# The last output projection of a two-layer mixer with tokens as rows: 512 channels per matmul, x turned beforehand, the final norm's weights spread by DMA, and the result sent in two halves of tokens

## The chip, the core and the metric

The kernel runs on one core of one Trainium2 chip. The metric is the device time of one execution in microseconds (us). Three executions of the kernel before took 1207.74, 1208.77 and 1210.25 us; their median, 1208.77 us, is the time before. The profile and the trace come from another execution, which took 1207.9 us.

TensorE (PE) does the matmuls and transposes, VectorE (DVE) and ScalarE (ACT) the element-wise work, GpSimd (POOL) a few powers, and SyncE (SP) issues all DMA transfers. Each engine takes its instructions in the order in which the program wrote them.

## The reference, cut to what matters

```python
def rms_norm(x, w):
    y = x * lax.rsqrt(jnp.mean(x * x, axis=-1, keepdims=True) + NORM_EPS)
    return y * w

def hybrid_layer(x, ...):               # x: 256 tokens x 1024 channels, float32
    h = rms_norm(x, norm_w)
    z = h @ w_in + b_in                 # 20 x 1024 columns: queries, keys, values, gates, convolution
    ...                                 # retention -> y_ret, attention -> y_att, convolution -> y_conv
    merged = gates[0] * y_ret + gates[1] * y_att + gates[2] * y_conv
    return x + merged @ w_out

for l in range(2):
    x = hybrid_layer(x, ...)
return rms_norm(x, final_norm_w)
```

## The kernel before, in words

All products run in a split form: a float32 matrix is taken apart into a high part and a low part, and a product is the sum of three matmuls (high by high, high by low, low by high). The weights arrive in steps of 256 output columns, 96 steps in each layer and 192 in all (`units`, numbered n). A step is named here by its kind and number: the last layer ends with ma2, ma3, then ya0 to ya3 (attention's projection), mc0 to mc3 (a merge gate), cg0 to cg3, yc0 to yc3 (the convolution's projection) and wo0 to wo3 (the output projection `w_out`), steps 164 to 191.

For each step three things are written into the program at different places. `load(n + 3)` stands at the head of step n and lets SP issue the transfer of the weights of step n + 3 into two `raw` tiles (there are five). `split(n + 2)` comes next: ACT casts each raw tile into `whi`, DVE subtracts and writes `wlo` (five of each). Then come the matmuls of step n. So a raw tile is free for a later load when DVE has written the `wlo` of what lay in it. What follows the matmuls is set by tables of due times: `play(inside, n)` in the middle of a step's matmuls, `play(first, n)` and `play(due, n)` behind them. Kinds in `WIDE` are taken two steps at a time (`gemm_wide`): tokens are the rows of the result, 128 at a time, and a matmul yields 512 channels; the first of the two steps covers contraction blocks 0 to 3 and the second 4 to 7, each first for tokens 0 to 127 (t = 0) and then for tokens 128 to 255 (t = 1). 

One dependence crosses these steps. The layer norm of the convolution needs its mean over channels: DVE works out `mean` and two diagonal matrices `dg` during ya3, behind the splits of mc0 and mc1 in DVE's order, and PE multiplies by them in the middle of mc0 (`ln_rows`, the matmul that writes `rb`).

The residual `x` has channels as rows (`xt`, 8 blocks of 128 channels by 256 tokens). The output projection, in both layers, yields channels as rows too (`gemm_two`): 256 columns a matmul. `project_last` adds it to x, multiplies by the final norm's weights (a number for each row here), and `turn_out` transposes the product back to tokens as rows, for the first four blocks in the middle of wo3 and for the others behind it. The sums of squares over channels are matmuls against a column of ones (`token_sums`), one part behind wo3; `rstd` follows on DVE and POOL; ACT and DVE scale the four 128 x 512 pieces of the result, and SP sends each.

Of the kernel before, what the change touches and what calls it, by code (L numbers as in the profile page):

```python
# [10 lines left out]
F32 = mybir.dt.float32  # L11
# [15 lines left out]
W = 256  # L27
# [117 lines left out]
def trunk(ctx: ExitStack, tc, xp, wp, b_in, params, consts, out):  # L145
# [78 lines left out]
    def bank():  # L224
        return ps.tile([128, 2, W], F32, tag="g", name="g", bufs=4)
# [33 lines left out]
    def gemm_wide(n, a, done):  # L259

        hs, ls = hi_t.pop(n), lo_t.pop(n)
        n0, half = couple[n]
        if half == 0:
            st["wide"] = [bank(), bank()]
        for t in range(2):
            p = st["wide"][t]
            if t == 1:
                play(inside, n)
            r = slice(t * 128, t * 128 + 128)
            for c in range(4):  # L270
                k, d = 4 * half + c, slice(2 * (c % 2), 2 * (c % 2) + 2)
                wh, wl = hs[c // 2][:, d, :], ls[c // 2][:, d, :]
                for i, (u, v) in enumerate(((0, wh), (0, wl), (1, wh))):
                    PE.matmul(p, a[:, k, u, r], v, start=(k == 0 and i == 0), stop=(k == NK - 1 and i == 2))  # L274
            if half and t == 0:
                done(0, p)
        return p

    def gemm_two(n, a, done):


        hs, ls = hi_t.pop(n), lo_t.pop(n)
        n0, half = couple[n]
        if half == 0:
            whole = bank(), bank()
            st["two", n0] = [halves(t) for t in whole], whole
            if n0 + 2 == N:
                st["two", n0][0][1][1] = ps.tile([128, W], F32, tag="S", name="g", bufs=4)
        parts, whole = st["two", n0]
        for u in range(2):  # L290
            if u == 1:
                play(inside, n)
            last = n0 + u + 1 == N
            for j, c in ((j, c) for j in range(2) for c in range(4)) if last else ((j, c) for c in range(4) for j in range(2)):
                k, d, t = 4 * half + c, 2 * (c % 2) + u, slice(j * 128, j * 128 + 128)
                for i, (w, v) in enumerate(trio_of(a, k, hs[c // 2][:, d, t], ls[c // 2][:, d, t])):
                    PE.matmul(parts[u][j], w, v, start=(k == 0 and i == 0 and (j == 0 or last)),  # L297
                              stop=(k == NK - 1 and i == 2 and (j == 1 or last)))
            if half and u == 0:
                done(0, whole[0])  # L300
        return parts[1] if last else whole[1]

    def hi_lo(dst, k, v, nk, n=None):

# [13 lines left out]
    def token_sums(tiles, ss=None, more=False):  # L318

        start = ss is None  # L320
        if start:
            ss = ps.tile([128, 2], F32, tag="S", name="ss", bufs=4)
        for q, v in enumerate(tiles):
            for t in range(2):
                PE.matmul(ss[:, t:t + 1], v[:, t * 128:t * 128 + 128], ones[:, 0:1],
                          start=(start and q == 0 and t == 0), stop=(not more and q == len(tiles) - 1 and t == 1))
        return ss
# [381 lines left out]
        later(pos[l + 1, "cs", 0], add_squares, (l + 1, "sq"), xs, i == 0, i == 3, at=first)  # L709


    def turn_out(k):
        if k == 0:
            st["nat"] = [[ps.tile([128, 512], F32, tag="S", name="nat", bufs=4) for _ in range(2)]]
        if k == 4:
            st["nat"].append([bank().rearrange("p a b -> p (a b)") for _ in range(2)])
        for t in range(2):
            PE.transpose(st["nat"][k // 4][t][:, (k % 4) * 128:(k % 4) * 128 + 128],
                         st["xf"][:, k, t * 128:t * 128 + 128], ident)

    def early_sums(l):
        st["ss"] = token_sums([st.pop((l, "sq"))], more=True)

    def project_last(l, i, p):

        if i == 0:
            st["xf"] = sb.tile([128, NK, S], F32, tag="cacc", name="xf", bufs=1)
        k = 2 * i
        if i < 3:
            DVE.tensor_tensor(x[:, k:k + 2], p, x[:, k:k + 2], ALU.add)  # L730
            add_squares((l + 1, "sq"), x[:, k:k + 2], i == 0, i == 2)
        sqs = []
        for j in range(2):
            if i == 3:
                DVE.tensor_tensor(x[:, k + j], p[j], x[:, k + j], ALU.add)
                sq = sb.tile([128, S], F32, tag="pts1", name="sq")
                ACT.activation(sq, x[:, k + j], AF.Square)
                sqs.append(sq)
            DVE.tensor_scalar(st["xf"][:, k + j], x[:, k + j], prm[:, P_FINAL + k + j:P_FINAL + k + j + 1], None, ALU.mult)
            if i < 2:  # L740
                later(N - 1, turn_out, k + j, at=inside)
        if i < 3:
            return
        early_sums(l + 1)
        turn_out(4)
        turn_out(5)
        r = rstd(token_sums(sqs, st["ss"]), NORM_EPS)
        turn_out(6)
        turn_out(7)
        for half in range(2):  # L750
            for t in range(2):
                o = sb.tile([128, 512], F32, tag="gt", name="o", bufs=4)
                if t == 0:
                    ACT.mul(o, st["nat"][half][t], r[:, t:t + 1])
                else:
                    DVE.tensor_scalar(o, st["nat"][half][t], r[:, t:t + 1], None, ALU.mult)
                SP.dma_start(out[t * 128:t * 128 + 128, half * 512:half * 512 + 512], o)


    def finish(n, p):  # L760
# [14 lines left out]
    def finish_half(n, t, p):  # L775

        l, kind, i = units[couple[n][0]]
        if kind in ("rv", "av"):
            wide_values(l, kind, i, t, p)
        elif kind in ("mr", "ma", "mc"):  # L780
            merge_gate(l, i, kind, t, p)
        elif kind != "wo":
            branch(l, i, ("r", "a", "c").index(kind[1]), n, t, p)
        elif l + 1 < DEPTH:
            project(l, i + t, n, p)
        else:
            project_last(l, i + t, p)

    held = []

# [5 lines left out]
    for l in range(DEPTH):  # L796
        for i in (0, 1, 2, 3):
            b = pos[l, "rq", i - i % 2]
            later(b + 3 + 2 * (i % 2), ret_scores, l, i)
            later(b + 6 + 2 * (i % 2), ret_out, l, i, at=first)  # L800
            later(b + 8 + 2 * (i % 2), ret_back, l, i, at=first)
        for pair in range(4):
            b = pos[l, "aq", pair]
            v = pos[l, "av", pair]
            for g in range(3):
                later(b + 2 * g + 3, att_scores, l, pair, g)
            later(v + 1, att_exp, l, pair)
            later(v + 2, att_share, l, pair)
            later(v + 4, att_turn, l, pair, 0, 0, at=first)
            later(v + 4, att_turn, l, pair, 0, 1, at=first)  # L810
            later(v + 5, att_pv, l, pair, 0, at=first)
            later(v + 5, att_turn, l, pair, 1, 0, at=first)
            later(v + 5, att_turn, l, pair, 1, 1, at=first)
            later(v + 6, att_pv, l, pair, 1, at=first)
        for part in range(2):
            later(pos[l, "yr", 3], by_residue, l, part, 0)
            later(pos[l, "cs", 3], by_residue, l, part, 4)
        y, c = pos[l, "ya", 0], pos[l, "mc", 0]
        later(y + 1, ln_add, l)
        later(y + 3, ln_mean, l, at=inside)  # L820
        later(c + 0, ln_rows, l, at=inside)
        later(c + 0, ln_apply, l, ALU.add, (0, 2), at=first)
        later(c + 0, ln_square, l, (0, 2), at=first)
        later(c + 1, ln_apply, l, ALU.add, (4, 6), at=first)
        later(c + 1, ln_square, l, (4, 6), at=first)
        later(c + 3, ln_rstd, l, at=inside)
        later(c + 4, ln_rows, l, at=inside)
        later(c + 4, ln_apply, l, ALU.mult, (0, 2), at=first)
        later(c + 4, ln_apply, l, ALU.mult, (4, 6))
        b = pos[l, "cs", 0]  # L830
        later(b + 1, norm_diag, l, at=inside if l else first)
        later(b + 2, norm_rows, l, at=inside)
        later(b + 2, finish_held, at=inside)
        for d, ks in H:
            later(b + d, scaled, l, ks)

    def warm_up():

# [10 lines left out]
    with tc.manual_schedule():  # L849
# [24 lines left out]
        for n, (l, kind, i) in enumerate(units):  # L874
# [22 lines left out]
            else:  # L897
                src = st[l, "g" if kind in ("cs", "cl") and i < UNSCALED else "h"]
            if n in couple:
                p = (gemm_two if kind == "wo" else gemm_wide)(n, src, lambda t, p: finish_half(n, t, p))  # L900
            elif kind == "av":
                p = gemm_values(n, src)
            else:
                p = gemm(n, src)
# [62 lines left out]
```

## Time and profile before

| | |
|---|---|
| three executions, median (lowest to highest) | 1208.77 us (1207.74 to 1210.25) |
| the profiled execution, its own time | 1207.9 us |
| its span in the trace | 1206.0 us |
| PE busy | 1194.5 us, 99% of the span |
| DVE busy | 975.7 us, 81% |
| ACT busy | 750.9 us, 62% |
| bytes by DMA | 214.60 MB, 178 GB/s on average |

The span is the time from the first instruction to the last in the trace; the execution's own time is 1.9 us longer. A busy share is an average over the whole span. PE is the engine that is almost never idle, so its order of work is what the other engines have to keep up with.

### The profile page before, as it was taken

What the parts mean: (1) busy time and instruction counts of PE and PEld (TensorE: products, weight loads), DVE (VectorE), ACT (ScalarE), POOL (GpSimd) and SP (SyncE); (2) the same over time, 40 slices, a digit from 0 to 9 for tenths busy, and PEclk for the clock granted to TensorE, in tenths of its full rate; (3) what the DMA queues carried; (4) which work ended last, traced back from release to release, by engine and by line L of the source; (5) the groups of instructions that cost most, each with busy time, mean ns of one, the idle gap of its engine ahead of it and who ended that gap; (6) DMA issues with size and microseconds to landing.
All of it is one profiled execution on the core that took longest, in us unless ns stands there. A gap on an engine that the chain in (4) does not pass through costs nothing.

```text
span 1206.0 us, 21474 instructions
## 1 busy us (share of the span) xinstructions
PE 1194.5 (99%) x8260; PEld 1113.6 (92%) x8260; DVE 975.7 (81%) x1702; ACT 750.9 (62%) x1116; POOL 9.2 (1%) x17
## 2 busy tenths in 40 slices
PE   8999999999999999999999999999999999999997
PEld 8999989999999989888999989899999999898987
DVE  6978799888888887677689788998888878767775
ACT  6635466868686856456465446586767776664652
POOL 0000000000000000000000000000000000000000
PEclk9999999999999999999999999999999999999999
DMA  8764566554545566656546464655555555666560
GB/s 295 244 196 127 171 199 198 172 186 145 184 153 177 155 198 185 191 186 187 190 136 197 151 201 132 216 186 178 174 162 167 167 175 159 198 185 184 181 195 36
DMA packets 129910, 214.60 MB, mean 178 GB/s; under 512 B 9872, under 2 KB 99728, under 8 KB 129680
## 3 DMA queue, kind: packets, MB, share of 16 engines
q1 hardware_dynamic: 129808, 213.24, 56.3%
q8 instruction: 64, 1.05, 0.4%
q14 instruction: 38, 0.31, 0.1%
HBM read 212.15 MB, written 1.05 MB: 177 GB/s over the span
## 4 chain that ended last, share of the span: by engine, by line
PE 91%; issue 6%; DVE 1%; DMA 1%; ACT 1%; SPq 0%; POOLq 0%; POOL 0%; DVEq 0%
PE g L240 47%; PE g L274 31%; PE g L255 4%; PE as L589 2%; PE g L297 2%; PE u L641 1%; PE pt L623 1%; DMA raw<-in_wp 1%; PE rs L528 1%; PE u L636 1%; ACT whi L220 0%; PE rs L530 0%; PE u L637 0%; PE rt L560 0%; PE r L540 0%
## 5 line engine op out<-in xcount | busy, mean ns | idle before, releaser
L221 DVE TENSOR_TENSOR wlo<-raw,whi 128x1024 fp32r<-128x1024 f32 (+1 forms) x387 | 455.8, 1211 | 104.2 <-ACT whi L220 97.0
L220 ACT CAST whi<-raw 128x1024 fp32r<-128x1024 f32 (+1 forms) x387 | 391.5, 1042 | 198.6 <-PE g L274 126.0
L240 PE MATMUL g<-h,whi 128*128 128x256 f32 x1664 | 300.6, 283 | 0.0
L240 PEld LDWEIGHTS g<-h,whi 128*128 128x128 f32 x1664 | 256.8, 189 | 0.8
L240 PE MATMUL g<-h,wlo 128*128 128x256 f32 x832 | 234.8, 282 | 0.0
L240 PE MATMUL g<-hp,whi 128*128 128x256 f32 x1280 | 233.9, 285 | 0.0
L432 DVE SCALAR_TENSOR_TENSOR cacc<-cpad,prm,cacc 128x256 f32<-128x256 f32 x480 | 201.1, 477 | 0.5 <-ACT cacc L429 0.4
L240 PEld LDWEIGHTS g<-hp,whi 128*128 128x128 f32 x1280 | 200.3, 192 | 0.9
L240 PE MATMUL g<-hp,wlo 128*128 128x256 f32 x640 | 181.1, 283 | 0.0
L274 PE MATMUL g<-whi,h 128*128 128x512 f32 x512 | 165.4, 397 | 0.0
L240 PEld LDWEIGHTS g<-h,wlo 128*128 128x128 f32 x832 | 156.7, 188 | 0.0
L240 PEld LDWEIGHTS g<-hp,wlo 128*128 128x128 f32 x640 | 122.7, 192 | 0.0
L274 PE MATMUL g<-whi,gated 128*128 128x512 f32 x384 | 120.9, 391 | 0.0
L274 PEld LDWEIGHTS g<-whi,h 128*128 128x128 f32 x512 | 96.5, 188 | 21.8
L274 PE MATMUL g<-wlo,h 128*128 128x512 f32 x256 | 101.0, 394 | 0.0
L274 PEld LDWEIGHTS g<-whi,gated 128*128 128x128 f32 x384 | 72.1, 188 | 14.9
L274 PE MATMUL g<-whi,hp 128*128 128x512 f32 x256 | 82.3, 393 | 0.0
L499 DVE TENSOR_TENSOR zz<-zz,cst 128x512 f32<-128x512 f32 x48 | 33.2, 692 | 52.2 <-ACT zz L498 52.2
L274 PE MATMUL g<-wlo,gated 128*128 128x512 f32 x192 | 74.8, 390 | 0.0
L240 PE MATMUL g<-gx,whi 128*128 128x256 f32 x384 | 71.3, 286 | 2.9 <-ACT whi L220 1.9
L496 ACT ACTIVATE z<-g,prm 128x256 f32<-128x256 f32 x96 | 45.7, 476 | 29.7 <-PE g L240 12.7
L240 PEld LDWEIGHTS g<-gx,whi 128*128 128x128 f32 x384 | 60.1, 192 | 4.2 <-ACT whi L220 2.3
(156 smaller groups left out, 1520.9 us busy)
## 6 DMA issues: line engine op xcount, KB each, us to landing
raw<-in_wp SPq DMA_DIRECT2D x222, 512.0 KB, 4.9
raw<-in_wp SPq DMA_DIRECT2D x323, 256.0 KB, 4.3
bb<-in_b_in SPq DMA_DIRECT2D x56, 128.0 KB, 4.3
cst<-in_consts SPq DMA_DIRECT2D x1, 1408.0 KB, 9.7
out_y<-o SPq DMA_DIRECT2D x4, 256.0 KB, 2.4
xt<-in_xp SPq DMA_DIRECT2D x3, 256.0 KB, 5.2
cst<-in_consts SPq DMA_DIRECT2D x1, 384.0 KB, 7.1
prm<-in_params SPq DMA_DIRECT2D x1, 360.0 KB, 5.3
```

The source lines that it names most:

```text
L220: ACT.copy(h, t)
L221: DVE.tensor_tensor(lo, t, h.bitcast(F32), ALU.subtract)
L240: PE.matmul(p[:, j], w, v, start=(k == 0 and i == 0 and j == 0), stop=(k == NK - 1 and i == 2 and j == 1))
L255: PE.matmul(p[:, j], a[:, k, u, r], v, start=(k == 0 and i == 0 and j == 0), stop=(k == NK - 1 and i == 2 and j == 1))
L274: PE.matmul(p, a[:, k, u, r], v, start=(k == 0 and i == 0), stop=(k == NK - 1 and i == 2))
L297: PE.matmul(parts[u][j], w, v, start=(k == 0 and i == 0 and (j == 0 or last)), stop=(k == NK - 1 and i == 2 and (j == 1 or last)))
L432: DVE.scalar_tensor_tensor(c[:, 2 * i + j], cp[:, j, t:t + S], col(l, P_TAP + (2 * i + j) * TAPS + t), c[:, 2 * i + j], ALU.mult, ALU.add)
L496: ACT.activation(z[:, j], p[:, j], AF.Identity, bias=b)
L499: DVE.tensor_tensor(zz, zz, two(cst[:, sin:sin + S]), ALU.mult)
L528: PE.matmul(s[:, 0:256], k[:, d, 0:128], q[:, d, :], start=(d == 0), stop=(d == 1))
L589: PE.matmul(s[:, r], q[:, j, t], k[:, j, t] if g else k[:, j, :], start=True, stop=True)
L623: PE.transpose(p[:, i, r * 128:r * 128 + 128], sm[:, r, o:o + 128], ident)
```

## The change

`gemm_two` is no longer used for the last layer's output projection. wo0 to wo3 there go through `gemm_wide`, with 512 channels a matmul and tokens as rows. For the addition, x has to have tokens as rows as well: `turn_x` transposes all of x once, behind rk0 of the last layer (step 103), by 16 transposes on PE and four copies on ACT, back into x's own place. The final norm's weights are now needed along a row, the same in all 128 partitions: `final_rows` transposes them on PE behind ya0 (step 172), copies them on ACT, gathers them into one row by eight DMA transfers and spreads that row over 128 partitions by seven more, each of which doubles the rows. `project_last` adds, squares with a running sum on ACT (`accum_out`), multiplies by the weights on DVE, and when a half of the tokens is complete works out its factor, scales its two pieces and sends them. The first half of the tokens is complete in the middle of wo3.

```diff
-            st["wide"] = [bank(), bank()]
+            st["wide", n0] = [bank(), bank()]
...
-    def turn_out(k):
...
-        for t in range(2):
-            PE.transpose(st["nat"][k // 4][t][:, (k % 4) * 128:(k % 4) * 128 + 128],
-                         st["xf"][:, k, t * 128:t * 128 + 128], ident)
...
+    xr = xt[:, 8:].rearrange("p (t c) -> p t c", t=2)
+
+    def turn_x():
+
+        ts = [[ps.tile([128, 512], F32, tag="S", name="xr", bufs=4) for _ in range(2)] for _ in range(2)]
+        for t in range(2):
+            for k in range(NK):
+                PE.transpose(ts[t][k // 4][:, (k % 4) * 128:(k % 4) * 128 + 128], x[:, k, t * 128:t * 128 + 128], ident)
+        for t in range(2):
+            for half in range(2):
+                ACT.copy(xr[:, t, half * 512:half * 512 + 512], ts[t][half])
+
+    def final_rows():
+
+        p = ps.tile([NK, 128], F32, tag="S", name="fp", bufs=4)
+        PE.transpose(p, prm[:, P_FINAL:P_FINAL + NK], ident)
+        row = sb.tile([NK, 128], F32, tag="nm8", name="row", bufs=1)
+        ACT.copy(row, p)
+        st["fw"] = sb.tile([128, D], F32, tag="vw", name="fw", bufs=1)
+        for k in range(NK):
+            SP.dma_start(st["fw"][0:1, k * 128:k * 128 + 128], row[k:k + 1])
+        for e in range(7):
+            SP.dma_start(st["fw"][1 << e:2 << e], st["fw"][0:1 << e])
+
+    def project_last(i, t, p):
+        d = slice(i * W, i * W + 512)
+        xs = xr[:, t, d]
+        DVE.tensor_tensor(xs, p.rearrange("p a b -> p (a b)"), xs, ALU.add)
         if i == 0:
-            st["xf"] = sb.tile([128, NK, S], F32, tag="cacc", name="xf", bufs=1)
...
+            st["ss", t] = sb.tile([128, 2], F32, tag="sm2", name="ss", bufs=4)
+        ss = st["ss", t]
+        ACT.activation(sb.tile([128, 512], F32, tag="tmp", name="sq"), xs, AF.Square, accum_out=ss[:, i // 2:i // 2 + 1])
+        o = st["o", t, i] = sb.tile([128, 512], F32, tag="gt", name="o", bufs=4)
+        DVE.tensor_tensor(o, xs, st["fw"][:, d], ALU.mult)
+        if i == 0:
+            DVE.tensor_scalar(ss[:, 0:1], ss[:, 0:1], 1.0 / D, NORM_EPS, ALU.mult, ALU.add)
             return
...
+        r = sb.tile([128, 2], F32, tag="sm2", name="r", bufs=4)
+        DVE.scalar_tensor_tensor(r[:, 0:1], ss[:, 1:2], 1.0 / D, ss[:, 0:1], ALU.mult, ALU.add)
+        POOL.tensor_tensor(r[:, 1:2], r[:, 0:1], mhalf[:, 0:1], ALU.pow)
         for half in range(2):
...
+            o = st["o", t, 2 * half]
+            if half:
+                DVE.tensor_scalar(o, o, r[:, 1:2], None, ALU.mult)
+            else:
+                ACT.mul(o, o, r[:, 1:2])
+            SP.dma_start(out[t * 128:t * 128 + 128, half * 512:half * 512 + 512], o)
...
+    later(pos[DEPTH - 1, "rq", 0] + 1, turn_x)
+    later(pos[DEPTH - 1, "ya", 0], final_rows)
...
-                p = (gemm_two if kind == "wo" else gemm_wide)(n, src, lambda t, p: finish_half(n, t, p))
+                p = (gemm_two if kind == "wo" and l + 1 < DEPTH else gemm_wide)(n, src, lambda t, p: finish_half(n, t, p))
```

On SP the order before, from the loads of ma2 on, is this. `raw<-in_wp` is a piece of weights (four to a step), `bb<-in_b_in` a bias row, `out_y<-o` the result.

```order
L199 DMA raw<-in_wp 128x2x256 x24
L508 DMA bb<-in_b_in 128x256 x2
```

In the changed kernel the same stretch reads as follows. The eight pieces ahead are the loads of ya2 and ya3, the sixteen behind are those of mc0 to mc3.

```order
L199 DMA raw<-in_wp 128x2x256 x8
L730 DMA fw<-row 1x16x8 x8
L732 DMA fw<-fw 1x16x64
L732 DMA fw<-fw 2x1024
L732 DMA fw<-fw 4x1024
L732 DMA fw<-fw 8x1024
L732 DMA fw<-fw 16x1024
L732 DMA fw<-fw 32x1024
L732 DMA fw<-fw 64x1024
L199 DMA raw<-in_wp 128x2x256 x16
L504 DMA bb<-in_b_in 128x256 x2
```

Fifteen transfers have come between the loads of ya3 and those of mc0. The first needs ACT's copy of the row, and each of the last seven needs the one ahead of it (the first of the seven all eight rows) to have landed.

On DVE the program ends like this before, from the first piece of the output projection on (`xt` is x, `xf` x times the final weights, `nat` the transposed product).

```order
L730 TENSOR_TENSOR xt<-g,xt 128x512
L739 TENSOR_SCALAR xf<-xt,prm 128x256 x2
L730 TENSOR_TENSOR xt<-g,xt 128x512
L362 TENSOR_TENSOR acc<-acc,sq 128x512
L739 TENSOR_SCALAR xf<-xt,prm 128x256 x2
L730 TENSOR_TENSOR xt<-g,xt 128x512
L362 TENSOR_TENSOR acc<-acc,sq 128x512
L330 TENSOR_TENSOR acc<-acc 128x256
L739 TENSOR_SCALAR xf<-xt,prm 128x256 x2
L735 TENSOR_TENSOR xt<-g,xt 128x256
```

In the changed kernel DVE's last ten rows, for channels 512 to 1023 with the second half of the tokens behind the first, begin with the end of the earlier piece.

```order
L745 TENSOR_SCALAR ss<-ss 128x1
L737 TENSOR_TENSOR xt<-g,xt 128x512
L743 TENSOR_TENSOR o<-xt,fw 128x512
L748 SCALAR_TENSOR_TENSOR r<-ss 128x1
L753 TENSOR_SCALAR o<-o,r 128x512
L737 TENSOR_TENSOR xt<-g,xt 128x512
L743 TENSOR_TENSOR o<-xt,fw 128x512
L748 SCALAR_TENSOR_TENSOR r<-ss 128x1
L753 TENSOR_SCALAR o<-o,r 128x512
```

The scaling of the first tokens' piece (L753, which waits for POOL's power) now stands ahead of the addition for the second tokens.

On PE the 16 transposes of x stand between rk0 and rq1 (the second and third of these rows).

```order
L240 MATMUL g<-h,whi 128x256 x2
L240 MATMUL g<-h,wlo 128x256
L717 MATMUL xr<-cst,xt 128x128 x16
L240 MATMUL g<-h,whi 128x256 x2
L240 MATMUL g<-h,wlo 128x256
```

Nothing but these 16 has been put there; before, the matmuls of rq1 followed those of rk0 at once.

## Rows read from the trace of the kernel before

**Rows 1.** The page of the profile: busy time of each engine with its share of the span and its count of instructions.

```profile
PE 1194.5 (99%) x8260; PEld 1113.6 (92%) x8260; DVE 975.7 (81%) x1702; ACT 750.9 (62%) x1116; POOL 9.2 (1%) x17
```

**Rows 2.** Busy time by stretch: from and to, length, then busy us and count for PE, its weight loads, DVE, ACT, POOL; then PE's granted clock, the DMA engines' share and GB/s. The first stretch is step ya0, the second wo0 to wo3.

```profile
1080.78:1086.22 5.44, 5.44 (x25) 4.50 (x24) 3.62 (x5) 4.44 (x5) 0.00 (x0) 1.00 0.57 175
...
1172.89:1197.45 24.56, 24.56 (x209) 24.55 (x208) 15.73 (x25) 7.16 (x10) 0.00 (x0) 1.00 0.05 16
```

**Rows 3.** SP's issues in order of time, from windows of 1 us (start, length, queue, line, what): the loads of mc0, one row for each of its two raw tiles. Then one row of SP's own waits: in total, times, longest.

```profile
1081.98 0.88 SPq L199 DMA_DIRECT2D raw<-in_wp  x2
...
1086.04 0.88 SPq L199 DMA_DIRECT2D raw<-in_wp  x2
...
SPq L199 <- DVE wlo L221: 77.7, 37, 6.4
```

**Rows 4.** The instructions around the transfers of the result and, from 1075 to 1110 us, of the weights: length in ns and first and last start of SP's four issues of the result, and the time from issue to landing for the result (256 KB each) and for the weights (256 KB each).

```profile
L757 SPq DMA_DIRECT2D out_y<-o x4: 360/393/406, 1201.0 to 1202.4; - x4
...
DMA to landing us min/median/max: 2.1/2.4/2.7
...
DMA to landing us min/median/max: 3.1/4.3/6.3
```

**Rows 5.** PE in order of time around the end of ya0 (the pair at 1085.99 is the last matmul of ya0 and the first of ya1), at the start of mc0 (1103.05) and in its middle.

```profile
1085.99 0.62 PE L274 MATMUL g<-whi,gated 128*128 128x512 f32 x2
...
1103.05 0.40 PE L274 MATMUL g<-whi,h 128*128 128x512 f32 x1
...
1106.04 0.68 PE L352 MATMUL rb<-dg,cst 128*128 128x128 f32 x4
```

**Rows 6.** DVE in order of time from the splits of mc0 and mc1 to the diagonals; in brackets idle time ahead and what ended it.

```profile
1097.82 3.49 DVE L221 TENSOR_TENSOR wlo<-raw,whi 128x1024 fp32r<-128x1024 f32 x3
1102.95 1.23 DVE L221 TENSOR_TENSOR wlo<-raw,whi 128x1024 fp32r<-128x1024 f32 x1 [1.64 <-ACT whi L220]
1104.09 0.68 DVE L681 TENSOR_TENSOR mg<-g,mg 128x512 f32<-128x512 f32 x1
1104.81 0.69 DVE L682 TENSOR_TENSOR m<-m,mg 128x512 f32<-128x512 f32 x1
1105.42 0.15 DVE L447 TENSOR_SCALAR mean<-ss 128x2 f32<-128x2 f32 x1
1105.61 0.48 DVE L346 TENSOR_SCALAR dg<-cst,mean 128x128 f32<-128x128 f32 x2
```

**Rows 7.** ACT in order of time behind rk0's eviction in the last layer, up to that of rq1 (`z` at 656.60). The last two rows are groups over the whole span (count, busy us, mean ns).

```profile
651.58 1.05 ACT L220 CAST whi<-raw 128x1024 fp32r<-128x1024 f32 x1
653.58 1.05 ACT L220 CAST whi<-raw 128x1024 fp32r<-128x1024 f32 x1 [0.96 <-PE g L240]
656.60 0.84 ACT L482 ACTIVATE z<-g,prm 128x256 f32<-128x256 f32 x2 [1.96 <-PE g L240]
...
L625 ACT COPY pts<-pt 128x512 f32<-128x512 f32 x32 | 17.5, 598 | 0.0
...
L381 ACT COPY rows<-rb 128x256 f32<-128x256 f32 x2 | 0.7, 370 | 1.8 <-PE rb L352 1.8
```

**Rows 8.** PE in order of time around the eight transposes in the middle of wo3.

```profile
1193.01 0.40 PE L297 MATMUL g<-mh,whi 128*128 128x256 f32 x2
1193.25 0.28 PE L297 MATMUL g<-mh,wlo 128*128 128x256 f32 x1
...
1193.73 1.04 PE L718 MATMUL nat<-cst,xf 128*128 128x128 f32 x8
1194.52 0.48 PE L297 MATMUL g<-mh,whi 128*128 128x256 f32 x2
1194.84 0.28 PE L297 MATMUL g<-mh,wlo 128*128 128x256 f32 x1
```

**Rows 9.** The end of the program on all engines in order of time, from the last matmul of wo3 on.

```profile
1197.33 0.28 PE L297 MATMUL g<-mh,wlo 128*128 128x256 f32 x1
...
1197.65 0.42 DVE L735 TENSOR_TENSOR xt<-g,xt 128x256 f32<-128x256 f32 x1
...
1199.27 0.16 DVE L338 TENSOR_SCALAR v<-ss 128x2 f32<-128x2 f32 x1 [0.81 <-PE ss L325]
1199.51 0.69 POOL L340 TENSOR_TENSOR r<-v,mhalf 128x2 f32<-128x2 f32 x1 [70.29 <-DVE v L338]
1200.24 0.75 DVE L756 TENSOR_SCALAR o<-nat,r 128x512 f32<-128x512 f32 x1 [0.81 <-POOL r L340]
...
1200.95 1.83 SPq L757 DMA_DIRECT2D out_y<-o  x4
```

**Rows 10.** Groups by line and shape (count, busy us, mean ns, idle ahead): the addition to x on DVE and the square on ACT from 1060 us on, and over the whole span the instruction that ACT adds behind an activation with a running sum.

```profile
L730 DVE TENSOR_TENSOR xt<-g,xt 128x512 f32<-128x512 f32 x3 | 2.1, 692 | 3.1 <-PE g L297 3.1
...
L360 ACT ACTIVATE sq<-xt 128x512 f32<-128x512 f32 x2 | 1.3, 634 | 4.4 <-DVE xt L730 4.4
...
L604 ACT ACTIVATION_READ_ACCUMULATOR Sm<-Sm,nm 128x1 f32 x32 | 6.0, 186 | 0.0
```

**Rows 11.** PE's granted clock behind its last work (stretches as in rows 2), where PE's last matmuls start at 1199.10 and end by 1199.73.

```profile
1199.10 0.63 PE L718 MATMUL g<-cst,xf 128*128 128x128 f32 x4
...
1202.00:1202.50 0.50, 0.00 (x0) 0.00 (x0) 0.00 (x0) 0.00 (x0) 0.00 (x0) 1.00 1.01 377
...
1203.00:1204.00 1.00, 0.00 (x0) 0.00 (x0) 0.00 (x0) 0.00 (x0) 0.00 (x0) 0.50 1.02 381
```

More of the change, by code (lines that the diff above doesn't have):

```diff
@@ L263, in gemm_wide @@
         if half == 0:
-            st["wide"] = [bank(), bank()]
+            st["wide", n0] = [bank(), bank()]
         for t in range(2):
-            p = st["wide"][t]
+            p = st["wide", n0][t]
             if t == 1:
@@ L286, in gemm_two @@
             st["two", n0] = [halves(t) for t in whole], whole
-            if n0 + 2 == N:
-                st["two", n0][0][1][1] = ps.tile([128, W], F32, tag="S", name="g", bufs=4)
         parts, whole = st["two", n0]
@@ L292, in gemm_two @@
                 play(inside, n)
-            last = n0 + u + 1 == N
-            for j, c in ((j, c) for j in range(2) for c in range(4)) if last else ((j, c) for c in range(4) for j in range(2)):
+            for c, j in ((c, j) for c in range(4) for j in range(2)):
                 k, d, t = 4 * half + c, 2 * (c % 2) + u, slice(j * 128, j * 128 + 128)
                 for i, (w, v) in enumerate(trio_of(a, k, hs[c // 2][:, d, t], ls[c // 2][:, d, t])):
-                    PE.matmul(parts[u][j], w, v, start=(k == 0 and i == 0 and (j == 0 or last)),
-                              stop=(k == NK - 1 and i == 2 and (j == 1 or last)))
+                    PE.matmul(parts[u][j], w, v, start=(k == 0 and i == 0 and j == 0),
+                              stop=(k == NK - 1 and i == 2 and j == 1))
             if half and u == 0:
                 done(0, whole[0])
-        return parts[1] if last else whole[1]
+        return whole[1]
     def hi_lo(dst, k, v, nk, n=None):
@@ L709, in project @@
         later(pos[l + 1, "cs", 0], add_squares, (l + 1, "sq"), xs, i == 0, i == 3, at=first)
-    def turn_out(k):
[L713 to L716, printed above, removed]
-        for t in range(2):
-            PE.transpose(st["nat"][k // 4][t][:, (k % 4) * 128:(k % 4) * 128 + 128],
-                         st["xf"][:, k, t * 128:t * 128 + 128], ident)
@@ L721, in early_sums @@
-    def early_sums(l):
-        st["ss"] = token_sums([st.pop((l, "sq"))], more=True)
-    def project_last(l, i, p):
-        if i == 0:
-            st["xf"] = sb.tile([128, NK, S], F32, tag="cacc", name="xf", bufs=1)
[L728 to L742, printed above, removed]
-            return
[L744 to L749, printed above, removed]
-        for half in range(2):
-            for t in range(2):
[L752 to L757, printed above, removed]
@@ L786, in finish_half @@
         else:
-            project_last(l, i + t, p)
+            project_last(i, t, p)
     held = []
```

## The prediction

> **What bounds the kernel now.** I began with busy time by engine: PE works 99% of the span [rows 1]. So a change pays only where PE gets less to do, where the end behind its last matmul gets shorter, or where something makes PE wait. Then I read three stretches for those three questions. In the output projection PE is busy from first to last, 24.56 of 24.56 us [rows 2], so fewer or wider matmuls there count in full. Behind the last matmul of wo3, which ends at 1197.33 + 0.28 = 1197.61 [rows 9], the span has 8.39 us to run to 1206.0. And the orders in front of this text show that SP gets fifteen transfers between the loads of ya3 and of mc0, so I looked at what those loads feed. SP takes its list in order and blocks at a wait: 77.7 us of one load line's time is waiting for DVE to free raw tiles [rows 3]. mc0's two raw tiles are asked for at 1081.98 and 1086.04 [rows 3], and PE begins mc0 at 1103.05 [rows 5].
>
> The tightest place is in the middle of mc0. DVE splits mc0 and mc1 (until 1102.95 + 1.23 = 1104.18), does one product and one sum, then the mean and the diagonals, which end at 1105.61 + 0.48 = 1106.09 [rows 6]; PE's matmul on them starts at 1106.04 [rows 5]. It starts the moment they are there. So a split of mc1 that ends later moves PE one for one.
>
> **The change, part by part.**
>
> *x transposed once.* Eight transposes in wo3 take 1194.52 - 1193.73 = 0.79 us, and the pair of matmuls behind them 0.32 us instead of 0.24, so 0.08 more [rows 8]. Sixteen cost 2 x 0.79 + 0.08 = 1.66 us on a full PE. ACT's four copies, at the 598 ns of a 512-column copy, are 2.4 us [rows 7]; they push the cast of 651.58 back by about 2.7 us, but ACT is idle 0.96 and 1.96 us before its next two pieces of work [rows 7], which takes up 2.9. I price them at nothing; without that cover it is 2.4 us. The transpose of the final weights is 0.1 + 0.08, together 0.17 us.
>
> *512 channels a matmul.* ya0 is a step of this form: 24 matmuls in 5.44 us, 0.2267 us each [rows 2]. wo0 to wo3 become 96 x 0.2267 = 21.76 us. Two groups of four transposes of the merged input remain, (0.79 / 2 + 0.08) x 2 = 0.95. That is 22.71 for 24.56: 1.85 us saved, the eight transposes in wo3 among them. The last matmul itself is longer, 0.39 for 0.28 at its end: 0.11 lost. So the last matmul would end at 1197.61 + 1.66 + 0.17 - 1.85 + 0.11 = 1197.70 if nothing stalled.
>
> *The end.* Let E be the end of the last matmul. The first half of tokens is complete 12 x 0.2267 = 2.72 us ahead. Its chain is addition 0.69, square 0.64 and its running sum 0.19 [rows 10], factor 0.15, then from the end of DVE's small step to the scaled pieces' start 1200.24 - 1199.43 = 0.81 for POOL [rows 9], with some 0.1 of gaps: it starts scaling at E - 0.14 and DVE is free, after 0.7, at E + 0.55. Before, DVE's addition started 0.04 behind the matmul. So the first tokens do not leave ahead of E, and the second tokens' addition waits 0.5 us behind them. Then 0.69 + 0.03 + 0.64 + 0.19 + 0.03 + 0.15 + 0.81 + 0.69 brings its scaled pieces to E + 3.8, and SP issues two, the second at E + 4.27 (four starts from 1201.0 to 1202.4 give 0.47 each) [rows 4]. Before, the last issue started 3.6 us ahead of the span's end; that gives E + 7.87 for 8.39, 0.52 us saved.
>
> *The spread of the final weights.* This is the term that decides. In the clock of before: ya0's last matmul and ya1's first are the pair that starts at 1085.99 [rows 5], so the transpose between them would be done by 1086.5, and ACT's copy of 128 columns takes under the 0.37 of a 256-column one [rows 7], so SP's first row goes out at about 1086.95. Eight rows at 0.47 us put the last at 1090.25. Now each doubling waits for what lies ahead to land, so there are seven landings in a chain (the rows, then six doublings) before SP comes to mc0's loads. No row shows a small transfer inside the chip. From above, the result's pieces of 256 KB land in 2.1 to 2.7 us; from below, take 0.6 us off the 2.1 for moving 256 KB (at some 400 GB/s; rows 11 have 381): 1.5. I take 1.9, near the least of a landing seen, because all but the last doublings are far smaller, and 0.1 us for SP to go on: 2.0 a link. The last doubling is issued at 1090.25 + 14.0 = 1104.25 and mc0's first load at S = 1104.7, later than 1081.98 by 22.7 us. Here the Trainium skill speaks against the change too: its page "DMA: Bandwidth & Descriptors", section "Anatomy of one DMA", gives about 2.0 us fixed for a transfer plus its bytes over 436 GB/s. By it a link would be an estimated 2.15 us and the time below 1.0 us more; no run yet shows the small transfer.
>
> Behind S: eight pieces (mc0, mc1) at 0.47 go out by S + 3.3. mc0's first tile lands at S + 0.47 + 3.1 to 4.3 [rows 4] and is cast by S + 4.6 to 5.9, four subtractions follow at 3.49 / 3 = 1.16 [rows 6], so mc1's split ends at S + 9.3 to 10.6; the fourth tile, landing in 4.3 to 5.3, holds it to some S + 10.1. From that end to the matmul on the diagonals it is 1106.04 - 1104.18 = 1.86 [rows 5, 6]. I take S + 12.0 = 1116.7, for 1106.04: **a stall of 10.7 us**, part of it before mc0 and part in its middle. Behind it, what DVE, ACT and the loads have to do stands as before, so I expect no second stall and nothing regained. The loads of mc2, mc3 and the bias rows queue on SP behind mc1's and would land by S + 15; PE ends the first half of mc1, where the bias is first used, at about S + 12 + 2.7 + 2.7 = S + 17.4, and mc1 at S + 20, so they cost nothing more.
>
> *Sum.* 1206.0 + 1.66 + 0.17 - 1.85 + 0.11 - 0.52 + 10.7 = 1216.3 of span. With the 1.9 us outside it, 1218.2 against the profiled execution's 1207.9. The median of the three runs is 0.9 above that execution; I put half of this on: **1218.5 us**.
>
> **Rivals.**
>
> *Quick links (a smaller stall).* If a small transfer lands in 1.5 us, the chain is 7 x 0.4 = 2.8 shorter: 1215.7, and with the weights landing at the least of rows 4 1215. For it: the small size. Against: the fixed part of a landing is not seen apart.
>
> *The weights alone are late.* If DVE reaches the diagonals early enough, the stall is only that before mc0: S + 5.3 against 1103.05, 7.0 us, 1214.8. Against it: rows 6 have the diagonals behind both splits.
>
> *Longer links, or a slow clock behind the gap.* At 2.7 us a landing the chain is 5.6 longer: 1224. PE's granted clock is 1.00 until 2.8 us behind its last work and 0.50, the lower of its two levels (1.2 for 2.4 GHz), from 1203 us on [rows 11]. PE would stand idle for some 6 us before mc0, so its first matmuls may run at half speed. Twelve of them then take 5.4 for 2.7 us but end before the diagonals come; only if the second half of mc0 is slow too does it cost 2.7 us: 1221.2. The Trainium skill, "TensorE: Matmul & The Clock Gate", section "Why this matters for your kernels", says gaps between bursts drop the clock; the rows agree on a drop, and none shows its cost in mid-kernel.
>
> *The spread is hidden (not slower).* The loads could slip without harm if S + 12.0 were no later than 1106.04: S at 1094.0. Then the seven landings would have (1094.0 - 0.47 - 1090.25) / 7 = 0.47 us each. Nothing in rows 4 lands in under 2.1. The time would be 1218.5 - 10.7 = 1207.8, no measurable change.
>
> **How the numbers follow.** Forecast (1216.5 to 1221) 0.52; quick links 0.17; weights alone 0.10; longer links or slow clock 0.16; hidden 0.05. The middle four span 1214 to 1224; quick links with every other bound at its least reach 1212. Range 1212 to 1224. About 0.2%, 2.4 us, is what a measurement can tell here from no change. Only the hidden case lies within it, and only with another gain of 2 us would it be faster: faster 0.01, same 0.05, slower 0.94.
>
> **What would show it.** Right: in SP's order seven issues some 2 us apart, mc0's loads at about 1106 (all is 1.8 us later by then), PE idle ahead of mc0 and again in its middle, wo0 to wo3 in about 22.7 us, and 7.9 us from the last matmul to the end. Wrong: the loads of mc0 issued before 1096, or no gap on PE ahead of `rb`; or a stall at rq1 from ACT's copies. The forecast falls if small transfers land in far under 1.5 us or if the copies behind rk0 hold up a split.

## The result, and the profile after

The changed kernel takes 1225.43 us (median of four runs, 1224.9 to 1227.08); the kernel before takes 1208.53 beside it. The ratio is 1.0142 with a 95% interval of 1.013 to 1.0154: slower by 17 us. The forecast was 1218.5 us in a range from 1212 to 1224. The side was right, and so was the place; the size was too small by 6.9 us, and the measured time lies 1.4 us outside the range.

The span is 1223.1 us for 1206.0. The page answers [rows 1] with PE at 98%, and in its 40 slices PE's granted clock dips once, where PE stands still.

```profile
PE 1199.1 (98%) x8153; PEld 1112.1 (91%) x8153; DVE 974.6 (80%) x1697; ACT 753.4 (62%) x1124; POOL 9.6 (1%) x18
...
PEclk9999999999999999999999999999999999997999
```

SP's issues in order of time (start, length, line, what) show what came between the loads of ya3 and of mc0, for [rows 3].

```profile
1089.10 1.25 SPq L730 DMA_DIRECT2D fw<-row  x2
...
1093.55 0.59 SPq L730 DMA_DIRECT2D fw<-row  x1
1095.30 0.50 SPq L732 DMA_DIRECT2D fw<-fw  x1
1098.12 0.70 SPq L732 DMA_DIRECT2D fw<-fw  x1
1100.05 0.65 SPq L732 DMA_DIRECT2D fw<-fw  x1
...
1109.18 0.51 SPq L732 DMA_DIRECT2D fw<-fw  x1
1109.73 0.59 SPq L199 DMA_DIRECT2D raw<-in_wp  x1
```

Eight rows, then seven doublings with 1.9 to 2.8 us between the starts of two, and only then the first load of mc0. The chain of work that ended last runs through them, in order of time (start, length, what).

```profile
1106.94 2.22 DMA fw<-fw
1109.18 0.51 SPq L732
...
1113.68 6.71 DMA raw<-in_wp
...
1120.49 1.05 ACT whi L220
1121.57 1.23 DVE wlo L221
1122.80 0.61 DVE mg L677
...
1124.23 0.30 DVE dg L342
...
1124.66 0.68 PE rb L348 x4
```

The last doubling but one lands, SP issues the last and then the weights, the weights land, ACT casts, DVE subtracts, makes the diagonals, and PE goes on. PE in order of time has its two gaps there, in place of [rows 5]; in brackets is the idle time ahead and what ended it.

```profile
1116.03 0.79 PE L274 MATMUL g<-whi,h 128*128 128x512 f32 x1 [10.39 <-ACT whi L220]
...
1124.66 0.68 PE L348 MATMUL rb<-dg,cst 128*128 128x128 f32 x4 [2.23 <-DVE dg L342]
```

`rb` starts 18.62 us later than in [rows 5]. Of these 0.38 are there before the first changed instruction, 1.74 are the transposes of x and 0.1 that of the final weights; some 16.4 us are the stall. Of the stall 10.8 us lie ahead of mc0's first matmul and 5.6 between it and `rb`: the gap of 2.23 ahead of `rb`, a wait of 0.47 for the first `wlo`, and 2.9 by which the first half of mc0 is longer at the lower clock.

PE's granted clock (stretch, length, busy us and count of PE, its loads, DVE, ACT, POOL; clock; DMA share and GB/s) is at its lower level, 0.50, when mc0 begins, comes back near 1122.7, and falls once more near 1126.1, behind the second gap and when PE has work again.

```profile
1120.00:1122.00 2.00, 2.00 (x6) 1.42 (x5) 1.66 (x2) 1.12 (x3) 0.00 (x0) 0.50 1.04 335
1123.00:1124.00 1.00, 0.00 (x0) 0.00 (x0) 0.96 (x2) 0.03 (x1) 0.00 (x0) 1.00 0.93 249
...
1127.00:1128.00 1.00, 1.00 (x4) 0.81 (x3) 0.17 (x1) 0.78 (x1) 0.00 (x0) 0.50 0.73 272
...
1130.00:1131.00 1.00, 1.00 (x6) 0.82 (x5) 0.72 (x2) 0.84 (x2) 0.00 (x0) 1.00 0.50 139
```

And the end of the program, for [rows 9], in order of time (some rows of each engine).

```profile
1216.01 0.39 PE L274 MATMUL g<-whi,mh 128*128 128x512 f32 x1
...
1216.09 0.49 DVE L753 TENSOR_SCALAR o<-o,r 128x512 f32<-128x512 f32 x1 [0.73 <-POOL r L749]
1216.49 0.68 DVE L737 TENSOR_TENSOR xt<-g,xt 128x512 f32<-128x512 f32 x1
...
1218.26 0.55 POOL L749 TENSOR_TENSOR r<-r,mhalf 128x1 f32<-128x1 f32 x1 [2.21 <-DVE r L748]
...
1219.60 0.81 SPq L756 DMA_DIRECT2D out_y<-o  x2
```

From the end of the last matmul, 1216.40, to the end of the span it is 6.70 us; before it was 8.39. So the end, one of the parts that were meant to win, does win, and the spread of one small row of weights loses ten times as much.

### The profile page after: what moved, and what is told of

Same layout as the page of the kernel before. It is cut to its first block, busy times and chain, and to the rows that moved or that the text cites. A ratio compares the mean times of both kernels' runs of the same rounds, so it can differ in the third digit from the quotient of the medians.

```text
span 1223.1 us, 21280 instructions
## 1 busy us (share of the span) xinstructions
PE 1199.1 (98%) x8153; PEld 1112.1 (91%) x8153; DVE 974.6 (80%) x1697; ACT 753.4 (62%) x1124; POOL 9.6 (1%) x18
## 4 chain that ended last, share of the span: by engine, by line
PE 95%; DMA 2%; SPq 1%; DVE 1%; ACT 0%; issue 0%; POOLq 0%; POOL 0%; ACTq 0%
PE g L240 48%; PE g L274 33%; PE g L255 4%; PE as L585 2%; PE g L293 2%; PE u L637 1%; PE pt L619 1%; DMA fw<-fw 1%; DMA raw<-in_wp 1%; PE rs L524 1%; PE u L632 1%; SPq L730 0%; PE rb L348 0%; SPq L199 0%; PE rs L526 0%
## 5 line engine op out<-in xcount | busy, mean ns | idle before, releaser
L274 PE MATMUL g<-whi,h 128*128 128x512 f32 x512 | 168.4, 403 | 10.4 <-ACT whi L220 10.4
L274 PEld LDWEIGHTS g<-whi,h 128*128 128x128 f32 x512 | 98.4, 192 | 33.0 <-ACT whi L220 10.8
```

## The experiments

The theory: SP stands at the waits of its chain and issues mc0's weights too late; PE then stops twice, and works at half clock behind the stops. The rivals: the loss lies in other parts of the change; the transfers themselves hold up the weights on the DMA engines; the clock costs nothing; and, for the size, that not the landings but the number of issues, or the weights alone, set the stall.

### The block taken apart, the transfers kept

```diff
-        for k in range(NK):
-            SP.dma_start(st["fw"][0:1, k * 128:k * 128 + 128], row[k:k + 1])
-        for e in range(7):
-            SP.dma_start(st["fw"][1 << e:2 << e], st["fw"][0:1 << e])
+    for j in range(4):
+        later(pos[DEPTH - 1, "ya", 0] + 1 + j, row_part, 2 * j)
+    for e in range(7):
+        later(pos[DEPTH - 1, "ya", 0] + 5 + e, double, e)
```

> The changed kernel with its fifteen transfers no longer in one block: the eight rows two to a step from ya1 on, the seven doublings one to a step behind them, so that each has landed before SP comes to the next and no load waits. If the block on SP is the whole loss (two gaps on PE of 10.4 and 2.2 us and the rest of the shift at the diagonals, 16.4 us in all, and 1.5 us of half clock behind them), the time is 1225.4 - 16.4 - 1.5 = 1207.5 us, and PE has no gap ahead of mc0 or of rb. If other parts of the change (the transposes of x, the wider matmuls, the later end) cost more than they save, it stays above 1210 us.

Measured: 1207.59 us (eleven runs) beside 1208.33, ratio 0.9992 (0.9983 to 1.0001). PE's longest wait (line waited for: us in total, times, longest) and its `rb`:

```profile
PE g L240 <- ACT whi L220: 1.9, 1, 1.9
...
1107.98 0.68 PE L348 MATMUL rb<-dg,cst 128*128 128x128 f32 x4
```

This wait is at the program's start, and the kernel before has it there too (1.9 us in two pieces); PE has no gap ahead of mc0 or `rb`. So the block on SP is the whole loss of 17 us: with the same transfers between other loads it is gone to within 0.1 us of what was expected.

### The chain alone, in the kernel before

`final_rows` is put in as the changed kernel has it, and its place is the same:

```diff
+    later(pos[DEPTH - 1, "ya", 0], final_rows)
```

> The kernel before with the spread of the final weights alone added at its place behind ya0; what it makes is not used, and all else is as before. If the fifteen transfers are the loss, it costs the gaps, the half clock and one transpose: 1208.5 + 16.4 + 1.5 + 0.1 = 1226.5 us, slower than the changed kernel by what the other parts win. If the loss needs the other parts too (a PE that is further ahead, fewer buffers), it comes out below 1222 us.

Measured: 1225.77 us (1225.14 to 1226.28), ratio 1.0143 (1.0129 to 1.0157), 0.7 below what was expected. PE's waits are again a gap ahead of mc0 and one ahead of `rb`:

```profile
PE g L274 <- ACT whi L220: 9.1, 1, 9.1
PE rb L352 <- DVE dg L346: 2.4, 1, 2.4
```

The spread needs nothing else of the change to cost 17.4 us. By this run the other parts together save 1225.77 - 1225.43 = 0.3 us, by the one above 1208.33 - 1207.59 = 0.7; neither is clear of the noise.

### The same chain from another queue

```diff
-            SP.dma_start(...)      # all fifteen
+            POOL.dma_start(...)
```

> The changed kernel with the same fifteen transfers, in the same chain and from the same time on, but issued by POOL, which is idle there; SP's order is as in the kernel before. If what costs is SP standing at waits ahead of the weights, nothing waits any more and the time is that of the version with one transfer a step, 1207.6 us. If the transfers themselves hold up the weights on the DMA engines, or the chain is needed sooner than it ends, it stays above 1212 us. POOL's power for the convolution's norm stands behind the chain and is due about 40 us after its start; links of more than 4 us would delay it.

Measured: 1207.74 us (eleven runs) beside 1208.64, ratio 0.9994 (0.9985 to 1.0003). POOL in order of time, with its waits in brackets:

```profile
1097.09 0.49 POOL L732 DMA_DIRECT2D fw<-fw  x1 [4.05 <-DMA fw<-row]
...
1122.54 0.53 POOL L732 DMA_DIRECT2D fw<-fw  x1 [5.03 <-DMA fw<-fw]
1130.59 0.71 POOL L336 TENSOR_TENSOR r<-v,mhalf 128x2 f32<-128x2 f32 x1 [7.52 <-DVE v L334]
```

The chain is even slower here, up to 5.5 us a link, and its last doubling goes out at 1122.5; nobody but the chain itself waits for it, since POOL's power becomes due only later. So neither the transfers nor the DMA engines are at fault, only the queue in which the waits stand.

### The mean's diagonals ahead of mc1's split

```diff
-        later(y + 3, ln_mean, l, at=inside)
+        later(y + 2, ln_mean, l, at=first)      # last layer only
```

> The changed kernel with the convolution's mean and its diagonals of the last layer placed behind ya2's matmuls, that is ahead of the split of mc1 in DVE's order. If the second gap comes from the diagonals standing behind mc1's split, PE no longer idles 2.2 us ahead of rb, the clock does not fall a second time, and the time is 1225.4 - 2.2 - 1.5 = 1221.7 us with mc0's first matmul where it was. If the weights' landing alone sets the time, PE waits about as long at mc1 instead and it stays at 1225 us. On the kernel before it would cost PE some 0.8 us behind ya2, which lies ahead of the gap here.

Measured: 1219.9 us (1219.58 to 1220.47), ratio 1.0095 (1.0081 to 1.0109): 5.5 us less than the changed kernel, where 3.7 were expected. PE's waits:

```profile
PE g L274 <- ACT whi L220: 7.9, 1, 7.9
...
PE rb L348 <- DVE dg L342: 0.7, 1, 0.7
...
1115.20 0.79 PE L274 MATMUL g<-whi,h 128*128 128x512 f32 x1 [7.95 <-ACT whi L220]
1120.98 0.60 PE L348 MATMUL rb<-dg,cst 128*128 128x128 f32 x4
```

The gap of 2.2 us ahead of this `rb` is gone (its row has no bracket); the 0.7 us in the list is a wait of the second `rb`, at 1145.14, for the norm's other diagonals. `rb` starts 3.7 us earlier and the clock stays at 1.00 from 1120 on. So the diagonals behind mc1's split were the second part of the stall, as the forecast had it. Of the 3.7 us, 2.2 are the gap, 0.8 are mc0's first matmul, which starts that much earlier in this execution, and some 0.6 are the first half of mc0, which ends at the higher clock here. From `rb` to the end it is 97.7 us for 98.4: the half clock behind `rb` is gone, and the second `rb` gives 0.7 of it back. Together this is the 4.4 us between the two profiled executions; the medians differ by 5.5.

### Fewer landings, more transfers

```diff
-        for e in range(7):
-            SP.dma_start(st["fw"][1 << e:2 << e], st["fw"][0:1 << e])
+        for m in (1, 4, 16):
+            for j in range(1, 4):
+                SP.dma_start(st["fw"][j * m:j * m + m], st["fw"][0:m])
+        SP.dma_start(st["fw"][64:128], st["fw"][0:64])
```

> The changed kernel with a shorter chain of more transfers: behind the eight rows, three copies each of 1, 4 and 16 rows (they do not wait for one another) and one of 64, so ten transfers behind four landings in place of seven behind seven. If landings set the time at which SP comes back to the weights, three links of about 2.25 us go and three issues of 0.55 and their spacing come: mc0's first load goes out about 3.8 us earlier than 1109.7, and the time is 1225.4 - 3.8 = 1221.6 us. If SP's issues set it, it is later by 3 x 0.55 and the time is 1227 us.

Measured: 1223.28 us (1222.48 to 1223.64), ratio 1.012 (1.0106 to 1.0134): 2.1 us less than the changed kernel, for 3.8 expected. SP's last issue of the chain and the first of mc0, and PE:

```profile
1106.49 0.51 SPq L734 DMA_DIRECT2D fw<-fw  x1
1107.04 1.33 SPq L199 DMA_DIRECT2D raw<-in_wp  x2
...
1122.62 1.19 PE L348 MATMUL rb<-dg,cst 128*128 128x128 f32 x4 [4.12 <-DVE dg L342]
```

The loads go out 2.7 us earlier, though SP issues three transfers more: landings set the time, not issues. My price of a link was right for its wait but left out that three issues in a row take 0.6 us each before the last of them can land. Of the 2.7 us `rb` keeps 2.0, and behind it 0.8 is lost again: the second gap is 4.1 us here, the clock falls to 0.50 within it and comes back near 1127.3, and `rb` itself takes 1.19 us for 0.68.

### The last doubling later

```diff
-        for e in range(7):
+        for e in range(6):
...
+    later(pos[DEPTH - 1, "yc", 0], last_rows)      # the doubling e = 6
```

> The changed kernel with the last doubling (64 rows, 256 KB), for which SP does not wait before the weights, issued at yc0 instead. If it is only one issue, mc0's first load and everything behind it come 0.55 us earlier: 1224.9 us. If its 256 KB also lie ahead of mc0's weights on the DMA engines, the time from mc0's first load to the first cast falls from 5.2 to about 4.5 us too: 1224.2 us.

Measured: 1222.99 us (1221.88 to 1223.46), ratio 1.0118 (1.0104 to 1.0131): 2.4 us less than the changed kernel.

```profile
1106.33 0.53 SPq L732 DMA_DIRECT2D fw<-fw  x1
1106.91 1.11 SPq L199 DMA_DIRECT2D raw<-in_wp  x2
...
1122.14 1.19 PE L348 MATMUL rb<-dg,cst 128*128 128x128 f32 x4 [3.60 <-DVE dg L342]
```

My expectation had miscounted: the last doubling waits for the one ahead of it, so leaving it out saves that landing as well. What it tells is in the stretch behind. From mc0's first load to the first cast it is 4.9 us for 5.2, of the 4.5 that a full effect would give; from mc0's first load to `rb` it is 1122.14 - 1106.91 = 15.2 us here and 1124.66 - 1109.73 = 14.9 in the changed kernel; the 256 KB ahead of the weights are not what makes this stretch long.

### Work of no use in the gaps

```diff
+    later(pos[DEPTH - 1, "mc", 0] - 1, filler, 78)
...
+            later(c + 0, filler, 30, at=inside)      # last layer, ahead of ln_rows
```

> The changed kernel with matmuls of no use in PE's two gaps: 78 behind ya3 (about 9.3 us, the gap was 10.4) and 30 in the middle of mc0 ahead of rb. If the half clock behind the gaps costs time, PE is at full clock in mc0 and mc1, the stretch from rb to the end shrinks by the 1.5 us that it had lost, and the time is 1223.9 us; the first half of mc0 is also quicker, which gains nothing, since rb waits for the diagonals. If the clock costs nothing, or the useless work itself delays mc0 or rb, it is 1225.4 us or more.

Measured: 1223.88 us (1223.01 to 1224.39), ratio 1.0125 (1.0112 to 1.0139), as expected. PE in order of time, and the clock where it was 0.50 before (columns as above):

```profile
1106.03 9.52 PE L726 MATMUL fill<-h 128*128 128x256 f32 x78
...
1125.14 0.60 PE L348 MATMUL rb<-dg,cst 128*128 128x128 f32 x4
...
1126.00:1128.00 2.00, 2.00 (x10) 1.60 (x10) 1.58 (x2) 0.81 (x1) 0.00 (x0) 1.00 1.04 330
```

`rb` starts 0.5 us later than in the changed kernel and the whole is still 1.6 us shorter. So the half clock behind `rb` costs 1.5 us or so, and the one ahead of it, in the first half of mc0, nothing: that half is quicker here, and `rb` is not earlier.

### The first 128 tokens held back

This kernel is the one with one transfer of the spread a step, with one more edit:

```diff
+        if t:
+            send_rows(0)
+            send_rows(1)
```

where `send_rows(t)` holds the factor, the scaling and the two issues that followed at once for each half.

> The version with one transfer of the spread a step, and with the first 128 tokens held back: their factor, scaling and sending stand behind the addition and the square of the second 128. If sending the first half ahead is worth what the chain behind the last matmul says (two powers, two scalings and four issues in a row behind it instead of one, one and two), the last issue of the result comes 1.4 us later and the time is 1207.6 + 1.4 = 1209.0 us. If it is hidden, the time is 1207.6 us.

Measured: 1208.48 us (eleven runs), 0.9 above the version without this edit; beside the kernel before the ratio is 1.0000 (0.9992 to 1.0009). SP's issues and DVE's last scaling:

```profile
1201.63 2.06 SPq L766 DMA_DIRECT2D out_y<-o  x4
...
1202.10 0.49 DVE L763 TENSOR_SCALAR o<-o,r 128x512 f32<-128x512 f32 x1 [0.67 <-POOL r L759]
```

In the traces the end is 7.97 us behind the last matmul for 6.72, 1.25 us more, which the expectation put at 1.4. By the traces the first half's early departure is worth about a microsecond; in the times alone, 0.9992 and 1.0000 with overlapping intervals, it is not clear of the noise.

### The spread without transfers, twice

```diff
+            DVE.tensor_scalar(fd[:, j], ident, prm[:, P_FINAL + k:P_FINAL + k + 1], None, ALU.mult)
...
+            PE.matmul(p[:, j * 128:j * 128 + 128], ones, st["fd", half][:, j], start=True, stop=True)
+        ACT.copy(st["fw"][:, half * 512:half * 512 + 512], p)
```

In the first form the diagonals and the matmuls stand together, in cg1 and cg2.

> The changed kernel without any transfer for the final weights: DVE makes eight diagonal matrices, PE multiplies a matrix of ones by them (eight 128x128 matmuls in steps cg1 and cg2), ACT copies the two banks. If SP's block is the whole loss, SP's order is as before and the time is that of the version with one transfer a step plus about 1.8 us of matmuls on a full PE, less 0.1 for the transpose that is gone: 1209.2 us. If the loss lies elsewhere it stays above 1215 us.

Measured: 1219.98 us (1219.21 to 1220.58), ratio 1.0095 (1.008 to 1.0111), 10.8 more than expected. PE's waits, and a stretch with its clock at 0.68:

```profile
PE fp L730 <- DVE fd L729: 6.0, 3, 3.9
...
1140.00:1150.00 10.00, 6.08 (x32) 5.65 (x32) 7.03 (x12) 6.38 (x10) 0.00 (x0) 0.68 0.44 130
```

I had moved the same fault to another engine: PE stood at its own head for matrices that DVE makes behind what is ahead of them in its order. These waits are 6.0 of the 10.8 us; the clock was at 0.50 behind them, which is the likely rest, but no run prices it here. In the second form DVE makes them in ya0 and ya1 and PE uses them in yc0 and yc1.

> The changed kernel without transfers for the final weights, as in the run with diagonals and a matrix of ones, but with the diagonals made on DVE in ya0 and ya1 and PE's eight matmuls in yc0 and yc1, so that PE waits for nothing there. If the 11 us of that run were PE waiting for diagonals that stood behind splits in DVE's order, it is gone and what is left is about 1.8 us of matmuls: 1209.2 us. If the matmuls themselves or their copies cost it, it stays near 1220 us.

Measured: 1209.26 us (eleven runs), ratio 1.0007 (0.9998 to 1.0016), as expected: the wait is gone, and two groups of four matmuls are left, of which one is below (the trace has two records for each of these matmuls).

```profile
1158.15 1.05 PE L733 MATMUL fp<-fd,cst 128*128 128x128 f32 x8
1158.96 0.48 PE L274 MATMUL g<-whi,gated 128*128 128x512 f32 x1
```

No version measured is clearly faster than the kernel before; the best two, 0.9992 and 0.9994, have 1 in their intervals.

## Why the prediction was right in kind and wrong in size

Three steps of the forecast failed. Two terms of its sum were too small by 2.9 us each: the chain of landings that leads to mc0's first load, and the stretch from that load to the diagonals. The third, the lower clock behind the stall, was put at nothing in the sum and cost 1.5.

*What bounds, and the place: right.* PE stopped ahead of mc0 and ahead of `rb`, for weights that SP had issued late, and the run with the transfers spread over the steps takes all of it back.

*The chain of landings (predicted 14.0 us from the last row to the last doubling, S = 1104.7 plus what the transposes shift).* Measured, mc0's first load goes out at 1109.73, which is 2.9 us later than the forecast when the measured shift ahead of it, 2.1, is added. Two prices were too small. The eight rows were priced at 0.47 us an issue, from the issues of the result; they take 0.64 from start to start, 1.2 us more in all. And a link was priced at 2.0; from the first doubling to the last it is (1109.18 - 1095.30) / 6 = 2.31, 1.9 us more; with the link behind the rows, 1.75, the mean of the seven is 2.23. The section of the Trainium skill that the forecast names ("DMA: Bandwidth & Descriptors", "Anatomy of one DMA") gives its fit for transfers that GpSimd issues, and these are issued by SP. The estimate worked out from it, 2.15 (with the 252 KB of the chain and the 0.1 for SP, 2.18), is 0.05 to 0.08 below the measured mean. The links show no steady growth with size: 1.93 for 8 KB, then 2.24 to 2.37 from 16 KB to 128 KB.

*From the first load to the diagonals (predicted 12.0 us).* Measured 14.93: the second term that failed, by 2.9 us. I took the landing of the weights from pieces that go out in pairs, 3.1 to 4.3 us, and 4.3 to 5.3 for the fourth tile. Behind the block all of mc0 and mc1 and the first of mc2 go out in one burst. The last piece that counts, the eighth, goes out 3.95 us behind the first, not 3.3, and takes 6.71 us to land, in the chain of work above. That the burst is why it takes so long is argued; no run sends fewer pieces at once, and the DMA engines move 206 GB/s on average from 1110 to 1116 and 350 only from 1116 to 1122. What follows was as forecast: mc1's split to `rb` takes 1124.66 - 1122.80 = 1.86 us, to the hundredth what [rows 5, 6] give. The run with the last doubling moved away leaves this stretch as long as it was, and the runs with the chain alone and with four links have it at 15.3 and 15.6.

*The clock (priced at nothing).* The forecast had the drop as a rival that costs up to 2.7 us if the second half of mc0 ran slow, and gave that, together with longer links, a chance of 0.16. It did: 3.4 us at 0.50 from 1126.1 on cost about 1.5, by the run with work in the gaps and by the trace. From `rb` to the next `rb`, the first row below in the changed kernel and the second in the kernel before, it is 25.1 us for 23.65.

```profile
1149.76 0.71 PE L348 MATMUL rb<-dg,cst 128*128 128x128 f32 x4
...
1129.69 0.68 PE L352 MATMUL rb<-dg,cst 128*128 128x128 f32 x4
```

The slow first half of mc0 cost nothing, as forecast, since `rb` waited anyway. The rule of the Trainium skill ("TensorE: Matmul & The Clock Gate", "Why this matters for your kernels") that long gaps between bursts drop the clock holds here: the trace has 0.50 behind a gap of 10.4 us. The shorter gap of 2.2 us was followed by 0.50 too.

*The transposes of x (predicted 1.66): right.* They start at 651.03 and the next matmul at 652.69, and the pair behind them loses 0.08: 1.74. ACT's copies held nothing up.

*512 channels a matmul (predicted 1.74 us saved, net of the longer last one): right in kind.* From wo0 to the end of the last matmul the shift falls by 1.35. A matmul came every 0.231 to 0.233 us there, not every 0.2267 as in ya0; why, no run shows.

*The end (predicted 0.52 us saved).* Measured 1.69. The chain of the first tokens was shorter than priced: POOL's power of one column takes 0.55 for 0.69, and DVE's scaling out of SBUF 0.49 for the 0.7 that I took from one out of PSUM. So it is over at 1216.58, and the second tokens' addition starts 0.09 us behind the last matmul, not 0.55. Some 0.2 more is gained by POOL's power and SP's issue in the second tokens' chain, and 0.5 behind SP's last issue: from there to the end it is 3.1 us, where the forecast took 3.6 from the kernel before. That the first tokens do not leave ahead of the last matmul held: their first issue is at 1216.83.

*The sum.* 10.3 us were predicted on the span. With 2.9 for the chain, 2.9 behind it, 1.5 for the clock, 0.4 for the wider matmuls, 0.1 for the transposes, -1.2 for the end and the 0.4 by which this execution was late from the start, it is 17.3; measured are 17.1. The forecast's own additions hold to within 0.1 us, save that 256 KB at 400 GB/s take 0.66 us, not 0.6, which only a lower bound of a link uses. The rivals "quick links" and "the weights alone" fell by the traces, "hidden" by the runs. Of "longer links, or a slow clock" the clock came true, at 1.5 of its 2.7 us; the links were longer, but at 2.2 to 2.3 us nearer to the forecast's 2.0 than to the rival's 2.8. The two prices should have been added to each other and to the forecast when the range was drawn, not set side by side. That the weights behind the block would land later than in pairs stood in no rival.

## What to carry to other kernels

Count a chain of dependent transfers by its landings, and see what else is queued behind its waits: fifteen transfers of 512 bytes to 256 KB cost 17 us here because the weights stood behind them on SP, and nothing when each had a step's time to land or when an idle engine issued them. When a queue has been held up, price what it then issues as a burst, not at the landing of a lone pair (here 6.7 us, not 3.1 to 5.3), and follow it to the tightest wait downstream, here a diagonal matrix that stood behind a split in another engine's order. Replacing such a wait by one on another engine gains little (5 of the 17 us here) unless what is waited for has been made well ahead.

## What the runs showed of the hardware that I had not expected

A tiny transfer can hold SP longer than a large one: 0.57 to 0.63 us for each row of 512 bytes, where a 512 KB load of weights mostly shows 0.33. The time from one doubling to the next, 1.9 to 2.4 us from 8 KB to 128 KB, hardly depends on the size; the 4 KB one ahead of them took 2.8, and 1.6 in the run with the chain alone. The same links issued by POOL among the weights' traffic took 2.0 to 5.5 us. This goes with the traffic and not with the queue: issued by SP one to a step, between the loads, the fifteen landed in 2.7 to 6.2 us (median 4.4), and in the block, while no weights were on their way, in 1.6 to 3.1 (median 1.7).

PE's granted clock, back at 1.00 near 1122.7 when mc0's first half had ended, fell to 0.50 at about 1126.1, when PE had been busy again since 1124.66 behind a gap of 2.2 us. At the end of the kernel before, it was still at 1.00 from 2.3 to 2.8 us behind the last work [rows 11].
